# Every third lower weight part on Pool instead of DVE, in the first two blocks of a three-block model

## The chip, the cores and the metric

The kernel runs on one core of a Trainium2 chip. TensorE (PE) multiplies matrices, VectorE (DVE), ScalarE (ACT) and GpSimd (Pool) do elementwise work, and SyncE (SP) issues most transfers. The metric is the device time of one execution in microseconds; a median of several runs is compared with another.

## The reference

256 tokens of width 1024 in float32 pass through three blocks. The first has a gated recurrence, causal attention and a gated feed-forward part; the second has two kinds of attention and a table lookup ("peer": for each token 128 rows of a table of 16,384 are gathered); the third has a long convolution and 16 experts. Cut to what matters here, the first block's products with weights are:

```python
u = jnp.einsum('bsd,de->bse', h, w_in[l])                # 1024 x 7168
merged = (gates[:, :, 0] * jnp.einsum('bsc,cd->bsd', ya, w_proj_rnn[l])
          + gates[:, :, 1] * jnp.einsum('bsc,cd->bsd', yb, w_proj_attn[l]))
x = x + jnp.einsum('bsd,de->bse', merged, w_out[l])
up = causal_dwconv(jnp.einsum('bsd,df->bsf', h, w_up[l]), ffn_conv_w[l], ffn_conv_b[l])
act = jax.nn.gelu(up) * jnp.einsum('bsd,df->bsf', h, w_gate[l])
x = x + jnp.einsum('bsf,fd->bsd', act, w_down[l])
```

The second block opens with `mod = jax.nn.silu(c) @ ada_w[l] + ada_b[l]` and has the same kind of products with its own `w_in`, `w_out` and `wq`; the third has a like vector from `mod_w`.

## The kernel before

A product with a float32 weight matrix is made of three products of a rounded type: each operand is split into an upper part (rounded to that type) and a lower part (what is left). A weight tile is 128 x 1024, 512 KB. `K.mm3` (lines 158 to 160) multiplies upper by upper, upper by lower and lower by upper, so one tile costs PE 24 matmuls of 256 columns or 12 of 512.

The tiles come through a ring of five (`RING`, tile name `wraw`), filled by SP in the order of one long list (`items`). An item is a weight tile or, spread between the weights, a tile of `ada_w` or `mod_w`, which DVE alone uses (lines 369 and 372: it is multiplied by a column and added up in a tile `mod`; line 357 ends such a sum after eight matmuls of line 355 on PE). `K._process` takes the next item. For a weight, ACT makes the upper part `whi` (line 108) and DVE the lower part, `wlo` = `wraw` - `whi` (line 112). Three pairs of parts are held (`SPLIT`); a pair comes free when PE has done with it, and a place of the ring when `wlo` or the sum of line 372 has been read from it. SP's next transfer for that place waits for it, and SP's queue is in order, so later transfers wait behind it.

`K.get` hands PE's code the next pair. Before it does, it calls `_process` until three pairs are there (one while `still` is set, at the ends of a block). In the steady state two are there and the third is made, so a tile is split two tiles ahead of its use. Then `get` runs what has been put off (`settle`: results taken from PSUM, convolutions, splits of activations) and one step of `bg`. Every engine runs its instructions in the order in which this code writes them.

Pool does little in the first two blocks: the second of the two tiles that `K.ahead` splits at four places (also line 112), two pairs of squares `qkT` = `qk` * `qk` in `qk_norm` (line 533), whose sums DVE takes at line 536 as steps of `bg`, and six additions into `x` (line 976). In the lookup behind the second block, Pool issues all gathers (line 1174).

The feed-forward loop of the first block does, for each of 11 steps, two tiles of `w_up`, two of `w_gate`, two of `w_down`; DVE runs a convolution (lines 752 and 755: `cv` from `up`), a product (line 760, from PSUM) and the lower part of `act` (line 269). In the other stretch that is spoken of below, the gates of the recurrence, DVE works on `xa`, `om` and the sums of `qkT`; line 516 is `xa` = (`th` + 1) * `xa`, line 514 ACT's `th`.

Of the kernel before, what the change touches and what calls it, by code (L numbers as in the profile page):

```python
# [39 lines left out]
class K:  # L40
# [5 lines left out]
    def __init__(self, ctx, tc, a):  # L46
        self.tc, self.nc, self.a = tc, tc.nc, a
        nc = tc.nc
        self.const = ctx.enter_context(tc.tile_pool(name="const", bufs=1))
        self.dram = ctx.enter_context(tc.tile_pool(name="dram", bufs=1, space=DRAM))  # L50
        self.ps = tc.alloc_tile_pool(name="ps", bufs=4, space=PSUM, reuse_waits="tile")
        self.x = self.const.tile([128, 2, 1024], F32, name="x")
        for t in range(2):
            nc.sync.dma_start(self.x[:, t], a["x"][t * 128:t * 128 + 128])
        self.ident = self.const.tile([128, 128], F32, name="ident")
        nc.scalar.dma_start(self.ident, a["ident"])
        self.cols = self.const.tile([128, NCOLS], F32, name="cols")
        nc.scalar.dma_start(self.cols, a["cols"])
        self.ones = self.const.tile([128, 128], F32, name="ones")
        nc.vector.memset(self.ones, 1.0)  # L60
        self.sums, self.sums_bufs = None, 2
        self.still = False
        self.consume_first = False
        self.bg = []
        self.post = []
        self.bg_rate = 1
        self.ring = tc.alloc_tile_pool(name="ring", bufs=self.RING, side="right", reuse_waits="tile")
        self.split_p = tc.alloc_tile_pool(name="splt", bufs=self.SPLIT, side="right", reuse_waits="tile")
# [45 lines left out]
    def get(self):  # L114

        n = self.loaded
        m = 1 if self.still else self.SPLIT
        if self.consume_first:
            self.settle()
        while self.done < len(self.items) and (not self.parts or self.done < n and len(self.parts) < m):  # L120
            self._process()
        self._load(self.done + self.RING)
        self.settle()
        for _ in range(self.bg_rate):
            if self.bg:
                self.bg.pop(0)()
        return self.parts.pop(0)
# [691 lines left out]
def block2(k, mod, M):  # L819
# [190 lines left out]
    p3 = [k.mm(), k.mm()]  # L1010
    k.rows_part(p3, yT, 2, 4)
    M.vectors(1)
    k.still = True
    k.rows_part(p2, yT, 3, 4)
    k.later(x_add, 1, 0, p2)
    k.rows_part(p3, yT, 3, 4)
# [1223 lines left out]
@with_exitstack  # L2240
def model_kernel(ctx: ExitStack, tc: tile.TileContext, a: dict, out: bass.AP):
    ctx.enter_context(tc.manual_schedule())
    k = K(ctx, tc, a)
    mod2, items2 = k.modulation(k.const, 2, k.col("c2", 0, 8), a["ada_w"], a["ada_b"])
    mod3, items3 = k.modulation(k.const, 3, k.col("c3", 0, 8), a["mod_w"], a["mod_b"])
    raw = items2 + items3
    k.start(plan1(a, raw[:40], raw[40:80]) + plan2(a, raw[80:]) + plan3(a))
    pc = tc.alloc_tile_pool(name="b2c", bufs=1, reuse_waits="tile")
    M = Columns(k, mod2, pc)
    block1(k, lambda: M.vectors(0))  # L2250
    pA = [tc.alloc_tile_pool(name="pA0", bufs=2, reuse_waits="tile")]
    normed_at = block2(k, mod2, M)
    pA.append(tc.alloc_tile_pool(name="pA1", bufs=2, reuse_waits="tile"))
    F = peer(k, mod2, pA, normed_at)
    block3(k, mod3, F, out)
    for z in pA[::-1] + [pc, k.ps]:
        z.release()
# [23 lines left out]
```

## Time and profile before

| | us |
|---|---|
| median of 3 runs | 2575.07 (2574.85 to 2579.13) |
| the profiled execution, whole | 2579.07 |
| its span in the profile | 2577.2 |
| first two blocks, up to the last addition into `x` | about 642 |
| first gather of the lookup | 674.5 |

| engine | busy us in the span | share |
|---|---|---|
| PE | 2063.1 | 80% |
| DVE | 1374.0 | 53% |
| ACT | 566.4 | 22% |
| Pool | 326.8 | 13% |

The shares are averages over stages that differ. Up to 640 us, PE and DVE are both busy nearly all the time. From 770 to 1,030 us the gathers of the lookup keep the DMA engines at about 420 GB/s, and from 1,675 us on the experts' weights do so at about 415 GB/s. DVE has almost nothing to do in the last 900 us. A time in the rows below counts from the start of the span.

### The profile page before, as it was taken

What the parts mean: (1) busy time and instruction counts of PE and PEld (TensorE: products, weight loads), DVE (VectorE), ACT (ScalarE), POOL (GpSimd) and SP (SyncE); (2) the same over time, 40 slices, a digit from 0 to 9 for tenths busy, and PEclk for the clock granted to TensorE, in tenths of its full rate; (3) what the DMA queues carried; (4) which work ended last, traced back from release to release, by engine and by line L of the source; (5) the groups of instructions that cost most, each with busy time, mean ns of one, the idle gap of its engine ahead of it and who ended that gap; (6) DMA issues with size and microseconds to landing.
All of it is one profiled execution on the core that took longest, in us unless ns stands there. A gap on an engine that the chain in (4) does not pass through costs nothing. (4 is left out here: it accounts for less than half of the span.)

```text
span 2577.2 us, 29437 instructions
## 1 busy us (share of the span) xinstructions
PE 2063.1 (80%) x11067; PEld 1200.5 (47%) x11067; DVE 1374.0 (53%) x2774; ACT 566.4 (22%) x998; POOL 326.8 (13%) x317
## 2 busy tenths in 40 slices
PE   8899999899797777788778797876776677676675
PEld 8699898787653232343333795321122111221221
DVE  8988788877778887998665888200000000000001
ACT  5654444455411111211110443000000000000000
POOL 0100000001224333233222123000000000000000
PEclk9999999999899999899889898688778878878788
DMA  7767688674699999999878448799999999999997
GB/s 261 232 219 259 207 308 302 229 260 145 263 381 421 421 421 419 368 371 387 315 297 340 108 137 314 290 415 414 415 415 414 414 415 415 415 414 417 415 414 290
DMA packets 188031, 860.85 MB, mean 334 GB/s; under 512 B 29945, under 2 KB 35121, under 8 KB 131057
## 3 DMA queue, kind: packets, MB, share of 16 engines
q1 hardware_dynamic: 137904, 578.19, 59.0%
q0 software_dynamic: 36864, 268.45, 25.8%
q10 hardware_dynamic: 13120, 12.32, 1.5%
q8 instruction: 88, 1.44, 0.2%
q14 instruction: 55, 0.44, 0.0%
HBM read 857.79 MB, written 1.10 MB: 333 GB/s over the span
## 5 line engine op out<-in xcount | busy, mean ns | idle before, releaser
L1927 DVE TENSOR_TENSOR xe<-mm,m 128x256 f32<-128x256 f32 x15 | 6.4, 425 | 602.4 <-PE mm L1925 602.4
L112 DVE TENSOR_TENSOR wlo<-wraw,whi 128x1024 fp32r<-128x1024 f32 x223 | 276.2, 1242 | 95.9 <-ACT whi L108 94.1
L108 ACT ACTIVATE whi<-wraw 128x1024 fp32r<-128x1024 f32 x228 | 239.5, 1056 | 177.9 <-PE mm L159 53.1
L1226 PE MATMUL ys<-G,diag 128*128 128x512 f32 x480 | 228.9, 617 | 50.7 <-DVE diag L1216 50.5
L1968 PE MATMUL mm<-K,xe 128*32 128x512 f32 x864 | 150.7, 697 | 78.9 <-DMA K<-in_moe_w_dram 78.9
L1968 PE MATMUL mm<-we,xe 128*32 128x512 f32 x864 | 146.9, 774 | 82.7 <-DMA we<-in_moe_w_dram 82.5
L158 PE MATMUL mm<-hTh,whi 128*128 128x256 f32 x608 | 173.2, 285 | 0.8 <-DVE hTl L306 0.8
L1226 PEld LDWEIGHTS ys<-G,diag 128*128 128x128 f32 x480 | 89.7, 195 | 178.7 <-issue 87.7
L160 PE MATMUL mm<-hTh,wlo 128*128 128x256 f32 x608 | 170.5, 280 | 0.0
L159 PE MATMUL mm<-hTl,whi 128*128 128x256 f32 x608 | 170.2, 280 | 0.0
L1200 DVE SCALAR_TENSOR_TENSOR G<-G,h 128x1024 f32<-128x1024 f32 x120 | 145.5, 1214 | 25.7 <-DMA G<-in_uv_dram,ids 25.3
L1226 PE MATMUL ys<-rowsS,diag 128*128 128x512 f32 x252 | 126.3, 641 | 36.3 <-DVE diag L1216 29.5
L1206 ACT ACTIVATE acts<-dots 128x2 f32<-128x2 f32 x128 | 26.0, 203 | 527.9 <-DVE G L1200 236.8
L1174 POOL DMA_INDIRECT G<-in_uv_dram,ids x120 | 115.4, 962 | 207.2 <-PE ys L1226 100.7
L1226 PE MATMUL ys<-rowsL,diag 128*128 128x512 f32 x168 | 96.5, 716 | 49.0 <-DVE diag L1216 48.6
L2035 DVE TENSOR_TENSOR ye<-mm,m 128x512 f32<-128x512 f32 x16 | 11.1, 692 | 213.9 <-PE mm L2029 213.9
L2071 POOL TENSOR_TENSOR x<-x,zT 128x512 f32<-128x512 f32 x1 | 1.6, 1551 | 962.7 <-ACT x L2070 962.7
L158 PEld LDWEIGHTS mm<-hTh,whi 128*128 128x128 f32 x608 | 115.4, 190 | 4.8 <-issue 2.0
L159 PEld LDWEIGHTS mm<-hTl,whi 128*128 128x128 f32 x608 | 116.2, 191 | 0.7
L1968 PEld LDWEIGHTS mm<-K,xe 128*32 128x32 f32 x864 | 22.8, 115 | 199.5 <-DMA K<-in_moe_w_dram 183.8
L160 PEld LDWEIGHTS mm<-hTh,wlo 128*128 128x128 f32 x608 | 115.3, 190 | 0.4 <-DVE wlo L112 0.2
L1968 PEld LDWEIGHTS mm<-we,xe 128*32 128x32 f32 x864 | 21.1, 121 | 202.4 <-DMA we<-in_moe_w_dram 181.1
(521 smaller groups left out, 4329.1 us busy)
## 6 DMA issues: line engine op xcount, KB each, us to landing
we<-in_moe_w_dram SPq DMA_DIRECT2D x160, 1024.0 KB
K<-in_moe_w_dram SPq DMA_DIRECT2D x122, 1024.0 KB
wraw<-in_moe_w_dram SPq DMA_DIRECT2D x100, 512.0 KB
K<-in_moe_w_dram SPq DMA_DIRECT2D x84, 512.0 KB
wraw<-in_w_in_dram SPq DMA_DIRECT2D x48, 512.0 KB
wraw<-in_ada_w_dram SPq DMA_DIRECT2D x48, 512.0 KB
wraw<-in_mod_w_dram SPq DMA_DIRECT2D x48, 512.0 KB
wraw<-in_w_qkv_dram SPq DMA_DIRECT2D x24, 512.0 KB
```

What stands on the lines that cost most here:

```text
L108: nc.scalar.activation(hi, raw, AF.Copy)
L112: (lower or nc.vector).tensor_sub(lo, raw, hi)
L158: nc.tensor.matmul(out, lhs[0], rhs[0], start=start, stop=False)
L159: nc.tensor.matmul(out, lhs[0], rhs[1], start=False, stop=False)
L160: nc.tensor.matmul(out, lhs[1], rhs[0], start=False, stop=stop)
L1174: nc.gpsimd.indirect_dma_start(out=z, out_offset=None, in_=a["uv"], in_offset=bass.IndirectOffsetOnAxis(ap=i[:, n % 16:n % 16 + 1], axis=0))
L1200: nc.vector.scalar_tensor_tensor(u, u, 1.0, h2[0], op0=ALU.mult, op1=ALU.mult, accum_out=dots[s][:, e:e + 1])
L1206: nc.scalar.activation(acts[s][:, e:e + 2], dots[s][:, e:e + 2], AF.Gelu)
L1226: nc.tensor.matmul(ys[0][:, 512 * j:512 * j + 512], d, rows[n][1][:, 1024 + 512 * j:1536 + 512 * j], start=n % 128 == 0, stop=n % 128 == 127)
L1927: nc.vector.tensor_mul(xe, p, m4.unsqueeze(2).to_broadcast([128, 8, 32]))
L1968: nc.tensor.matmul(p[32 * j:32 * j + 32], xe[:, c], w[j], start=c == 0, stop=c == 7)
L2035: nc.vector.tensor_mul(ye, p, m5)
```

## The change

`get` counts weight tiles, and when the count is a multiple of three and the tile is the third pair (split two tiles ahead), it has the lower part made by Pool. A flag turns this off near the end of the second block, before the lookup begins. The lines below the first edit move by one, those below `get` by five.

```diff
@@ -60,6 +60,7 @@
         self.still = False
+        self.turn, self.assist = 0, True
@@ -118,7 +119,11 @@
         while self.done < len(self.items) and (not self.parts or self.done < n and len(self.parts) < m):
-            self._process()
+
+            weights = self.items[self.done][1] is None
+            self.turn += weights
+            far = weights and self.turn % 3 == 0 and len(self.parts) == self.SPLIT - 1
+            self._process(lower=self.nc.gpsimd if far and self.assist else None)
@@ -1010,7 +1015,7 @@
     M.vectors(1)
-    k.still = True
+    k.still, k.assist = True, False
```

58 of the `wlo` instructions move from DVE's queue to Pool's; nothing else moves on any engine. They are 14 up to 160 us of the profile before, 13 from there to 297 us, 21 in the feed-forward part (297 to 487 us) and 10 in the second block.

Pool's queue around the squares of line 533, before (numbers behind a name tell tiles apart):

```order
L112 TENSOR_TENSOR wlo_137<-wraw_86,whi_136 128x1024
L533 TENSOR_TENSOR qkT_1000<-qk_700 128x1024 x2
L533 TENSOR_TENSOR qkT_1225<-qk_1001 128x1024 x2
L112 TENSOR_TENSOR wlo_3068<-wraw_2957,whi_3067 128x1024
L112 TENSOR_TENSOR wlo_5254<-wraw_5126,whi_5253 128x1024
```

The same place of Pool's queue after:

```order
L113 TENSOR_TENSOR wlo_900<-wraw_801,whi_899 128x1024
L113 TENSOR_TENSOR wlo_1005<-wraw_903,whi_1004 128x1024
L538 TENSOR_TENSOR qkT_1000<-qk_700 128x1024 x2
L113 TENSOR_TENSOR wlo_1082<-wraw_1008,whi_1081 128x1024
L113 TENSOR_TENSOR wlo_1155<-wraw_1085,whi_1154 128x1024
L538 TENSOR_TENSOR qkT_1225<-qk_1001 128x1024 x2
L113 TENSOR_TENSOR wlo_1269<-wraw_1158,whi_1268 128x1024
```

The first squares now stand behind `wlo_1005`, the second behind `wlo_1155`, and `wlo_1269` behind the second.

DVE's queue at the same place (about 89 to 102 us), before:

```order
L112 TENSOR_TENSOR wlo_945<-wraw_880,whi_944 128x1024
L516 SCALAR_TENSOR_TENSOR xa_210<-th_957,xa_210 128x512
L516 SCALAR_TENSOR_TENSOR xa_210<-th_968,xa_210 128x512
L516 SCALAR_TENSOR_TENSOR xa_210<-th_979,xa_210 128x512
L516 SCALAR_TENSOR_TENSOR xa_210<-th_990,xa_210 128x512
L112 TENSOR_TENSOR wlo_1005<-wraw_903,whi_1004 128x1024
L536 TENSOR_REDUCE qss_1010<-qkT_1000 128x8
L372 SCALAR_TENSOR_TENSOR mod_1024_870<-wraw_905,mod_t_81,mod_1024_870 128x1024
L112 TENSOR_TENSOR wlo_1028<-wraw_925,whi_1027 128x1024
```

And after:

```order
L521 SCALAR_TENSOR_TENSOR xa_210<-th_979,xa_210 128x512
L521 SCALAR_TENSOR_TENSOR xa_210<-th_990,xa_210 128x512
L541 TENSOR_REDUCE qss_1010<-qkT_1000 128x8
L377 SCALAR_TENSOR_TENSOR mod_1024_870<-wraw_905,mod_t_81,mod_1024_870 128x1024
L113 TENSOR_TENSOR wlo_1028<-wraw_925,whi_1027 128x1024
```

`wlo_1005` has left the queue, and the sum over `qkT_1000` stands right behind the work on `xa`.

DVE's queue in the feed-forward part (about 387 to 398 us), before:

```order
L112 TENSOR_TENSOR wlo_4180<-wraw_4068,whi_4179 128x1024
L760 TENSOR_TENSOR cv_4029<-cv_4029,mm_4094 128x512
L372 SCALAR_TENSOR_TENSOR mod_1024_4135<-wraw_4100,mod_t_83,mod_1024_4135 128x1024
L112 TENSOR_TENSOR wlo_4202<-wraw_4102,whi_4201 128x1024
L269 TENSOR_TENSOR actl_4187<-cv_4029,acth_4186 128x512
L372 SCALAR_TENSOR_TENSOR mod_1024_4135<-wraw_4143,mod_t_83,mod_1024_4135 128x1024
L112 TENSOR_TENSOR wlo_4227<-wraw_4145,whi_4226 128x1024
L372 SCALAR_TENSOR_TENSOR mod_1024_4135<-wraw_4183,mod_t_83,mod_1024_4135 128x1024
L112 TENSOR_TENSOR wlo_4260<-wraw_4205,whi_4259 128x1024
L112 TENSOR_TENSOR wlo_4293<-wraw_4207,whi_4292 128x1024
```

And after:

```order
L765 TENSOR_TENSOR cv_4029<-cv_4029,mm_4094 128x512
L377 SCALAR_TENSOR_TENSOR mod_1024_4135<-wraw_4100,mod_t_83,mod_1024_4135 128x1024
L113 TENSOR_TENSOR wlo_4202<-wraw_4102,whi_4201 128x1024
L274 TENSOR_TENSOR actl_4187<-cv_4029,acth_4186 128x512
L377 SCALAR_TENSOR_TENSOR mod_1024_4135<-wraw_4143,mod_t_83,mod_1024_4135 128x1024
L113 TENSOR_TENSOR wlo_4227<-wraw_4145,whi_4226 128x1024
L377 SCALAR_TENSOR_TENSOR mod_1024_4135<-wraw_4183,mod_t_83,mod_1024_4135 128x1024
L113 TENSOR_TENSOR wlo_4293<-wraw_4207,whi_4292 128x1024
```

`wlo_4180` and `wlo_4260` have gone to Pool; the rest keeps its order.

## Rows read from the trace of the kernel before

**Rows 1.** Stretch, busy us (x count) of PE, PEld, DVE, ACT, POOL, clock, DMA.

```profile
110.00:160.00 50.00, 44.55 (x337) 41.88 (x336) 47.82 (x63) 28.31 (x36) 5.02 (x2) 0.93 0.69 222
...
400.00:450.00 50.00, 49.21 (x351) 44.13 (x351) 44.95 (x52) 23.03 (x26) 0.00 (x0) 1.00 0.89 310
```

**Rows 2.** PE's waits up to 660 us: total us, times, longest us.

```profile
PE mm L355 <- DVE mod L372: 6.2, 3, 5.5
...
PE mm L159 <- DVE wlo L112: 3.1, 4, 1.2
...
PE mm L160 <- DVE wlo L112: 1.9, 2, 1.2
```

**Rows 3.** Groups by line and shape: busy us, mean ns, idle before.

```profile
L112 DVE TENSOR_TENSOR wlo<-wraw,whi 128x1024 fp32r<-128x1024 f32 x223 | 276.2, 1242 | 95.9 <-ACT whi L108 94.1 <-ACT acts L1206 1.2
...
L372 DVE SCALAR_TENSOR_TENSOR mod<-wraw,mod_t,mod 128x1024 f32<-128x1024 f32 x84 | 109.5, 1303 | 0.0
...
L112 POOL TENSOR_TENSOR wlo<-wraw,whi 128x1024 fp32r<-128x1024 f32 x4 | 11.0, 2748 | 376.6 <-ACT whi L108 219.2 <-DVE rsn L209 157.4
```

**Rows 4.** Timeline, Pool and DVE together: start us, us, engine, line.

```profile
121.66 5.02 POOL L533 TENSOR_TENSOR qkT<-qk 128x1024 f32<-128x1024 f32 x2 [27.74 <-PE mm L160]
...
122.08 2.85 DVE L112 TENSOR_TENSOR wlo<-wraw,whi 128x1024 fp32r<-128x1024 f32 x1
...
491.33 2.46 POOL L112 TENSOR_TENSOR wlo<-wraw,whi 128x1024 fp32r<-128x1024 f32 x1 [204.86 <-ACT whi L108]
...
491.49 3.39 DVE L372 SCALAR_TENSOR_TENSOR mod<-wraw,mod_t,mod 128x1024 f32<-128x1024 f32 x1
...
621.15 2.55 POOL L976 TENSOR_TENSOR x<-x,s 128x512 f32<-128x512 f32 x2 [127.36 <-DVE s L973]
...
621.65 0.47 DVE L306 SCALAR_TENSOR_TENSOR hT2l<-mm,cols,hT2h 128x256 fp32r<-128x256 f32 x1
```

**Rows 5.** Timeline around the first squares: Pool, ACT, DVE.

```profile
88.39 5.53 POOL L533 TENSOR_TENSOR qkT<-qk 128x1024 f32<-128x1024 f32 x2 [73.98 <-ACT qk L569]
...
94.56 1.57 ACT L514 ACTIVATE th<-mm,hb 128x256 f32<-128x256 f32 x4 [3.18 <-DVE xa L516]
96.00 2.96 ACT L108 ACTIVATE whi<-wraw 128x1024 fp32r<-128x1024 f32 x3
...
97.11 1.23 DVE L112 TENSOR_TENSOR wlo<-wraw,whi 128x1024 fp32r<-128x1024 f32 x1 [0.26 <-ACT whi L108]
98.25 1.21 DVE L536 TENSOR_REDUCE qss<-qkT 128x8 f32<-128x1024 f32 x1
```

**Rows 6.** PE's longest wait in the timeline, and the stretch behind it by busy time.

```profile
129.77 1.08 PE L355 MATMUL mm<-mod,ones 128*32 128x256 f32 x8 [5.45 <-DVE mod L372]
...
128.50:135.40 6.90, 5.63 (x29) 4.83 (x30) 6.87 (x10) 0.61 (x1) 0.00 (x0) 0.51 0.55 164
```

**Rows 7.** Timeline of the feed-forward part: ACT, DVE, SP's issues, PE.

```profile
386.11 2.01 ACT L108 ACTIVATE whi<-wraw 128x1024 fp32r<-128x1024 f32 x2 [2.44 <-PE ac L160]
...
387.20 1.23 DVE L112 TENSOR_TENSOR wlo<-wraw,whi 128x1024 fp32r<-128x1024 f32 x1 [2.06 <-ACT whi L108]
...
388.61 0.28 PE L160 MATMUL mm<-hTh,wlo 128*128 128x256 f32 x1
...
390.25 0.33 SPq L93 DMA_DIRECT2D wraw<-in_w_gate_dram  x1
...
394.99 1.06 ACT L108 ACTIVATE whi<-wraw 128x1024 fp32r<-128x1024 f32 x1 [4.01 <-DMA wraw<-in_w_gate_dram]
...
396.09 2.50 DVE L112 TENSOR_TENSOR wlo<-wraw,whi 128x1024 fp32r<-128x1024 f32 x2 [0.60 <-ACT whi L108]
...
397.34 1.60 SPq L93 DMA_DIRECT2D wraw<-in_w_up_dram  x2
...
397.37 0.39 PE L160 MATMUL mm<-hTh,wlo 128*128 128x256 f32 x1
```

**Rows 8.** Pool's first gather of the lookup in the timeline.

```profile
674.50 2.19 POOL L1174 DMA_INDIRECT early<-in_uv_dram,ids  x1 [26.51 <-DVE gz L1130]
```

## The prediction

> **What bounds the kernel now.** I read the busy time by stretch first. Up to 640 us PE is the engine that sets the pace: in the middle of the feed-forward part it is busy 49.2 of 50 us, with DVE at 45.0 beside it, and in the gates of the recurrence DVE, at 47.8 of 50, is the busier of the two and PE loses 5.5 us [rows 1]. Then I read what PE waits for. The waits that have to do with DVE's lateness are few: 6.2 us for a sum of `mod`, and 3.1 and 1.9 us for `wlo` [rows 2]. The longest single one is at 129.77 us, 5.45 us for a sum that stands in DVE's queue behind work that runs without a gap since 97 us; behind it PE's clock is granted at 0.51 (the 1.2 GHz level) for 6.9 us [rows 6], which costs some 3.4 us more. So a DVE that came sooner everywhere could give back 6.2 + 3.1 + 1.9 + 3.4, some 14 us, and no more, because everywhere else PE is at work.
>
> A microsecond gained or lost here reaches the end. The first gather is issued at 674.5 us after a wait for DVE's choice of rows [rows 8], which needs the result of the second block; the gathers and then the experts' transfers come one after the other behind it, and nothing among them runs to a clock of its own. I count every shift of PE's work before 640 us once, in full.
>
> **What the change moves, and the price of one.** 58 `wlo` leave DVE, at 1.24 us each (mean), 72 us of its queue. On Pool the same instruction takes 2.46 to 2.75 us [rows 3, 4]. Pool has room: 58 times 2.75 is 160 us of 640. The price lies elsewhere, in what DVE does meanwhile. At 122.08 us a `wlo` on DVE ran beside Pool's squares and took 2.85 instead of 1.24 us. At 491.49 a sum of `mod` ran beside a `wlo` on Pool and took 3.39 instead of 1.30. At 621.65 an instruction whose one input is in PSUM ran beside Pool's additions at 0.47 us, no longer than elsewhere [rows 3, 4]. So a DVE instruction that reads two SBUF tiles stands still behind Pool's, by 1.61 (2.85 - 1.24) to 2.09 us (3.39 - 1.30), and one that reads PSUM doesn't. Each moved `wlo` then saves DVE 1.24 us and costs it nothing to 2.09: between -1.24 and +0.85 us. In the queues shown with the change, most of what stands around a moved `wlo` reads two SBUF tiles: the other `wlo`, the sums of `mod`, the convolutions, line 516, the lower part of `act`. Where DVE is behind I take +0.4, from the lower of the two rows, which is the one where Pool had to let a DVE instruction finish first, as will be usual in a full queue.
>
> The Trainium skill, page "SBUF — State Buffer", section "Who interferes with whom", says that a DVE instruction with two SBUF inputs and a GpSimd instruction that reads SBUF exclude each other, and that the one that comes second blocks for the whole instruction of the first. By that rule a moved `wlo` would cost DVE up to the whole 2.46 to 2.75 us, +1.2 to +1.5 net, and by an estimate the sum of this text would come out some 11 us higher (14 moved before 160 us, 0.8 more each). The trace agrees in kind and shows somewhat less, 2.09 of 2.46 us [rows 4].
>
> A second price: Pool's part is ready 1.2 to 1.5 us later than DVE's where DVE would have begun at once, and the place in the ring comes free as much later. Behind it wait, in SP's queue, all later transfers.
>
> **Up to 160 us, 14 moved.** DVE is behind here, so the ledger of its queue up to the sum at 129.77 counts. The first squares on Pool now stand behind `wlo_1005`. Before, they ran at 88.39 and held up line 516, for which ACT waited 3.18 us at 94.56 [rows 5]. Without them there, the first `whi` of the row at 96.00 ends at about 93.8 instead of 97.1; Pool makes `wlo_1005` until 96.3 and the first half of the squares until 98.8, and DVE's sum over them, next in its queue, starts there, where it stood at 98.25 before: +0.55. What DVE saved by the moved `wlo` (97.11) and by the squares' absence it spends waiting for the squares. Their second half then holds the sum of `mod` behind: +1.2 (until 101.3, when it could start at 100.0). `wlo_1082` and `wlo_1155`: +0.4 each, rounded up to 0.9. `wlo_1269` stands on Pool behind the second squares (121.66 + 5.02), meets DVE's scans and the awaited sum, +1.6, while the `wlo` that it saves stands behind that sum. Together 4.2 us; I take **+3**, because some of these meetings will be missed. Bounds: -9 (the whole wait and the half clock gone, 5.45 + 3.4) and +6 (14 times 0.4).
>
> **160 to 297 us, 13 moved.** None of the six waits for `wlo` in rows 2 lies here, and PE works without a break; a part is made two tiles ahead, some 5.6 us at 2.8 us a tile, of which `whi` (1.06) and Pool (2.75) take 3.8. That cover hides Pool's extra 1.5: **0**, at most +1.
>
> **Feed-forward part, 21 moved.** Here the ring counts. One revolution can be followed in rows 7: a transfer issued at 390.25 has its `whi` start at 394.99, when it lands, its `wlo` starts at 396.09 and its place is refilled at 397.34, 7.1 us for five tiles. PE takes five tiles (3.1 weights, the rest being `ada_w` or `mod_w`) in 8.7 us at 2.8 us a weight (351 matmuls in 49.2 us, 20 to a weight on the average [rows 1]). That leaves 1.6 us a revolution. Each revolution will hold about one moved `wlo`, +1.2 to +1.5, and a DVE instruction behind it that loses 0.4 to 0.85: 1.6 to 2.35 against 1.6, so 0 to +0.75 each, 0 to +16 for all. Directly: the `wlo` at 387.20 would be ready at 389.66 to 389.95 instead of 388.43, where PE reads it at 388.61, so PE loses 1.05 to 1.35; the one at 396.09 is ready at 398.55 to 398.85, where PE reads it at 397.37, or about a microsecond later by then, so 0.2 to 0.7 more [rows 7]. Two more of the 21 are as tight; the other 17 leave Pool 2.7 us and more. I take 1 us for each of the four and a tenth for each of the others, **+6**.
>
> **Second block, 10 moved.** At two places PE already waits for a `wlo` that is late because its `whi` is (two of the six waits of rows 2): 1.2 us more at each, **+2**, between 0 and +3. At the other eight PE waits for no part. The flag lets Pool go before the lookup, so its gathers meet none of this.
>
> **The sum.** 3 + 0 + 6 + 2 = +11 us. Against the profiled execution's own 2579.07 us that is 2590; it lay 4.0 above the median of the runs, 2575.07, so the median after should be **2586 us**. The bounds together are -14 (rows 2 and 6 all returned, no new wait) and +26.
>
> **Rivals.** First, faster: DVE's relief wins. It does if Pool's work falls mostly where DVE reads PSUM, waits or has nothing to do. DVE's 94 us of waiting for `whi` before a `wlo` speak for this [rows 3]: a moved `wlo` no longer blocks what stands behind it. Against it: in the stretch where PE loses most, DVE does not wait. From about 0.85 us of blocking downward per moved `wlo` the ledger turns; then the wait at 129.77 shrinks below what lets the clock fall, and 8 to 14 us come back: about 2564.
>
> Second, no change: PE covers it all. It is so if the ring keeps 1.6 us a revolution and the gates come out even: 2575, give or take 5.
>
> Third, much slower: the ring becomes the bound of the whole feed-forward part. It decides from 1.6 us of delay per revolution; with every revolution paying 0.75 and DVE's queue paying its upper price of 0.85 before 160 us, 16 + 12 + 3, less what is counted in both, some +28: 2603. The page's rule named above leads the same way.
>
> **How the numbers follow.** A difference of 0.2% (5 us) is about what a measurement of this kernel can tell from none. The forecast (2581 to 2598) gets 0.51, the third rival 0.09, no change 0.21, faster 0.19. So slower 0.60, same 0.21, faster 0.19. For 8 in 10 the range has to take in no change and part of faster: 2566 to 2602; the forecast's own is 2581 to 2598.
>
> **What would show it.** `wlo` on Pool at 2.4 to 2.8 us, 62 of them. On DVE, sums of `mod` and `wlo` up to 640 us that last 2 to 3.4 us instead of 1.24 and 1.30, in numbers of the order of 40; DVE's busy time up to 640 us not lower by 72 us but about the same. DVE's sum of line 536 (now 541) idle before it, waiting for Pool. PE's wait for the sum of `mod` near 130 us at 7 to 9 us instead of 5.45, and the first gather at about 685 instead of 674.5 us. In the feed-forward part, SP's transfers waiting for Pool, and PE waits of a microsecond for Pool's `wlo`. I am wrong if DVE's instructions keep their durations (then Pool and DVE do not meet), or if the first gather comes before 674 us. I am wrong about the place, and perhaps right about the sign, if PE's waits behind 300 us do not grow.

## The result: slower by 0.95%, in the forecast's direction and about twice its size

The changed kernel took 2600.66 us (median of 4 runs, 2598.84 to 2603.48) against 2577.10 us of the kernel before (4 runs beside it, 2574.85 to 2579.37). The ratio is 1.0095, with a 95% interval of 1.0080 to 1.0109: some 24 us slower. Forecast were 11 us, a median of 2586. The range given for 8 chances in 10, 2566 to 2602, holds the result near its upper end; the forecast's own, 2581 to 2598, does not. The profiled execution took 2599.27 us.

Here are the groups of the changed kernel that answer to [rows 3], from the page of the profile (line, engine, operation, shapes, count | busy us, mean ns | idle before). Line 112 is now 113, line 372 is 377.

```profile
L113 DVE TENSOR_TENSOR wlo<-wraw,whi 128x1024 fp32r<-128x1024 f32 x165 | 222.8, 1355 | 77.8 <-ACT whi L109 76.0
L113 POOL TENSOR_TENSOR wlo<-wraw,whi 128x1024 fp32r<-128x1024 f32 x62 | 163.5, 2638 | 478.9 <-ACT whi L109 474.6
...
L377 DVE SCALAR_TENSOR_TENSOR mod<-wraw,mod_t,mod 128x1024 f32<-128x1024 f32 x84 | 141.7, 1686 | 8.3 <-DMA wraw<-in_mod_w_dram 6.2
```

DVE has 58 `wlo` less, yet the mean of those it keeps rose from 1242 to 1355 ns, and that of the sums of `mod` from 1303 to 1686. The engines' busy time in the whole execution (us, share of the span, instructions), of the kernel before and then of the changed one:

```profile
PE 2063.1 (80%) x11067; PEld 1200.5 (47%) x11067; DVE 1374.0 (53%) x2774; ACT 566.4 (22%) x998; POOL 326.8 (13%) x317
```

```profile
PE 2061.1 (79%) x11067; PEld 1201.0 (46%) x11067; DVE 1385.9 (53%) x2716; ACT 567.1 (22%) x998; POOL 477.0 (18%) x375
```

DVE has 58 instructions fewer and is busy 12 us longer. What PE waits for in that time, beside [rows 2] (waiting engine and line, releaser: us in total, times, longest):

```profile
PE mm L360 <- DVE mod L377: 9.2, 4, 7.4
PE mm L164 <- DVE wlo L113: 6.7, 3, 5.1
...
PE mm L165 <- DVE wlo L113: 4.3, 4, 3.1
PE mm L165 <- POOL wlo L113: 4.3, 6, 1.3
PE ac L164 <- DVE wlo L113: 3.8, 6, 1.5
...
PE mm L164 <- POOL wlo L113: 3.2, 2, 1.9
```

DVE's own instructions, more than Pool's, are what PE waits for longest. The place of the loss comes from setting the first use of each weight tile on PE in one trace beside the other's (PE's shift, one execution of each kernel). The changed kernel is behind by 1.7 us at 39 us (in the time of before), 3.5 at 66, 7.4 at 74.5, 11.1 at 104.5, 14.2 at 167; then nothing until 264, where it becomes 16.5; from 356 to 477 us it climbs from 17.2 to 26.0; it falls back to 23.2 behind 520 us. The first gather, [rows 8], is late by the same:

```profile
697.79 2.19 POOL L1179 DMA_INDIRECT early<-in_uv_dram,ids  x1 [26.51 <-DVE gz L1135]
```

### The profile page after: what moved, and what is told of

It is laid out like the page before. It is cut to its first block, busy times and chain, and to the rows that moved or that the text cites. A ratio compares the mean times of both kernels' runs of the same rounds, so it can differ in the third digit from the quotient of the medians.

```text
span 2597.5 us, 29443 instructions
## 1 busy us (share of the span) xinstructions
PE 2061.1 (79%) x11067; PEld 1201.0 (46%) x11067; DVE 1385.9 (53%) x2716; ACT 567.1 (22%) x998; POOL 477.0 (18%) x375
## 5 line engine op out<-in xcount | busy, mean ns | idle before, releaser
L113 DVE TENSOR_TENSOR wlo<-wraw,whi 128x1024 fp32r<-128x1024 f32 x165 | 222.8, 1355 | 77.8 <-ACT whi L109 76.0
L113 POOL TENSOR_TENSOR wlo<-wraw,whi 128x1024 fp32r<-128x1024 f32 x62 | 163.5, 2638 | 478.9 <-ACT whi L109 474.6
L377 DVE SCALAR_TENSOR_TENSOR mod<-wraw,mod_t,mod 128x1024 f32<-128x1024 f32 x84 | 141.7, 1686 | 8.3 <-DMA wraw<-in_mod_w_dram 6.2
L1231 PE MATMUL ys<-rowsL,diag 128*128 128x512 f32 x168 | 90.7, 679 | 48.4 <-DVE diag L1221 48.4
L2040 DVE TENSOR_TENSOR ye<-mm,m 128x512 f32<-128x512 f32 x16 | 11.1, 692 | 212.9 <-PE mm L2034 212.9
```

The source lines that it names most:

```text
L113: (lower or nc.vector).tensor_sub(lo, raw, hi)
L377: nc.vector.scalar_tensor_tensor(z, raw, th[:, ch:ch + 1], z, op0=ALU.mult, op1=ALU.add)
L1231: nc.tensor.matmul(ys[0][:, 512 * j:512 * j + 512], d, rows[n][1][:, 1024 + 512 * j:1536 + 512 * j], start=n % 128 == 0, stop=n % 128 == 127)
```

## Hold-ups: what they look like

Three places of the changed kernel's timeline, Pool's `wlo` first and DVE's instruction beside it second (start us, us, engine, line):

```profile
38.43 2.86 POOL L113 TENSOR_TENSOR wlo<-wraw,whi 128x1024 fp32r<-128x1024 f32 x1 [5.29 <-ACT whi L109]
...
38.94 3.43 DVE L377 SCALAR_TENSOR_TENSOR mod<-wraw,mod_t,mod 128x1024 f32<-128x1024 f32 x1
...
66.97 2.41 POOL L113 TENSOR_TENSOR wlo<-wraw,whi 128x1024 fp32r<-128x1024 f32 x1 [6.91 <-ACT whi L109]
...
67.04 2.89 DVE L274 TENSOR_TENSOR yRl<-xa,yRh 128x512 fp32r<-128x512 f32 x1
...
571.80 2.38 POOL L113 TENSOR_TENSOR wlo<-wraw,whi 128x1024 fp32r<-128x1024 f32 x1 [11.06 <-ACT whi L109]
...
572.26 1.95 DVE L884 TENSOR_SCALAR m<-m 128x2 f32<-128x2 f32 x1
```

The sum of `mod` takes 3.43 instead of 1.28 us; `yRl` 2.89 where it takes 0.68 alone, and ten instructions later in DVE's queue stands a `wlo` for which PE waits 3.13 us (at 76.09); an instruction on two columns takes 1.95 where it takes 0.17. I added up, over all DVE instructions that overlap one on Pool up to 655 us, the duration less the median of the same form elsewhere (for three `yRl`, the 0.68 us of the kernel before): 10.9 us before, 90.5 after, of which 29.7 up to 172 us (6.7 before), 17.3 up to 310 (2.1), 35.2 up to 520 (2.1), 8.3 behind that (0.0). 55 instructions lost more than half a microsecond (6 before). That is 80 us of new hold-up for 72 us of relief (58 times 1.24), 1.37 us for each moved `wlo`.

## The experiments

The theories: **hold-up** (Pool's long read stops DVE instructions that read SBUF), **lateness** (a part made by Pool is ready later, and PE and the ring wait for it), and **queue** (Pool's squares stand behind a `wlo`, and DVE waits for them). Differences are of medians, in us against the runs of the kernel before on the same chip; the 95% interval of the ratio stands beside it. In the expectations TensorE is PE, VectorE DVE and ScalarE ACT.

### Does the loss add up by stretches?

One line before the loop behind the first 165 us (`k.assist = False`) leaves the first 14 moved parts:

```
+    k.assist = False
     prob = {}
```

> Pool's help is switched off before the feed-forward part's and the second block's share: only the first 14 moved lower parts (up to about 165 us) stay on Pool. By the profile after, TensorE's weight tiles stand 14 us later there, and by the theory that each lower part on Pool holds up a VectorE instruction beside it, and that this delay is local and never given back, the kernel comes to +12 to +15 us on the kernel before. The rival that the delay is only moved (the stretches behind would have waited anyway, and after's loss comes from the feed-forward part) gives +0 to +5 us.

Measured: +12.9 us (1.0038 to 1.0065). PE's weight tiles stand 14.9 us behind at 167 us and 15.0 at 666: nothing is given back. The other run turns the flag on for the feed-forward part of the first block alone:

```
-        self.turn, self.assist = 0, True
+        self.turn, self.assist = 0, False
     acts = {}
+    k.assist = True
     for r in range(11):
...
     last()
-    k.still = True
+    k.still, k.assist = True, False
```

> Pool helps in the 21 tiles of the feed-forward part of the first block alone. Local and additive losses: +7 to +9 us on the kernel before (after's shift grows from 16.2 to 24.5 us there). The ring-bound theory of the prediction with its own sizes: +6. If after's loss in the feed-forward part hangs on the kernel having come late into it (a ring still empty from the first stretch): +0 to +3.

Measured: +8.4 us (1.0023 to 1.0050). The two together are 21 of the 24; the feed-forward part loses its share although the kernel comes into it on time.

### Hold-ups without relief, and lateness without hold-ups

DVE keeps every `wlo`; Pool does an idle subtraction beside it, in five pieces:

```
+        if lower is not None and beside:
+            for h in range(5):
+                a = hi[:, 192 * h:192 * h + 192].bitcast(F32)
+                lower.tensor_sub(self.idle, a, a)
+            lower = None
         (lower or nc.vector).tensor_sub(lo, raw, hi)
```

> VectorE keeps every lower part, and Pool does an idle subtraction of the same kind beside it at the same 58 places (five pieces of 192 columns that read the upper part twice, into a scratch tile that nothing reads). Nothing of the kernel waits for Pool's result; only VectorE's relief is missing. By the theory of hold-ups (Pool's long reads of SBUF stop VectorE's instructions that read SBUF): at least after's loss, +24 to +45 us on the kernel before, and VectorE instructions of 2 to 3.5 us beside Pool's pieces. By the theory of lateness (a lower part made by Pool is ready later, and TensorE and the ring wait for that): 0 to +5 us.

Measured: +32.4 us (1.0112 to 1.0143). No product needs Pool's pieces here and DVE has no relief, and PE loses more than in the changed kernel. The timeline shows how DVE is held up, Pool first:

```profile
50.05 5.17 POOL L117 TENSOR_TENSOR idle<-whi 128x192 f32<-128x192 f32 x4
...
49.52 1.00 DVE L280 TENSOR_TENSOR yRl<-xa,yRh 128x512 fp32r<-128x512 f32 x1
50.44 1.52 DVE L119 TENSOR_TENSOR wlo<-wraw,whi 128x1024 fp32r<-128x1024 f32 x1
51.88 1.52 DVE L383 SCALAR_TENSOR_TENSOR mod<-wraw,mod_t,mod 128x1024 f32<-128x1024 f32 x1
```

Four pieces, 0.51 us each when alone, take 5.17 us: one piece runs between each two DVE instructions. A `wlo` takes 1.52 instead of 1.22 us, and Pool's piece waits meanwhile. They take turns. But two other effects are in these 32 us, so the run shows that hold-ups cost PE time and not how much they cost alone. Pool's squares stand behind the pieces, and DVE and PE behind the squares:

```profile
103.91 3.74 POOL L544 TENSOR_TENSOR qkT<-qk 128x1024 f32<-128x1024 f32 x2
...
105.84 1.22 DVE L547 TENSOR_REDUCE qss<-qkT 128x8 f32<-128x1024 f32 x1 [4.60 <-POOL qkT L544]
...
110.23 0.80 PE L170 MATMUL mm<-wlo,hTh 128*128 128x512 f32 x1 [5.91 <-DVE wlo L119]
```

And ACT waits three times, 13.5 us in all, until the pieces have read the upper part whose place it needs.

The opposite: the part is as late as Pool would have it, but nothing long is read.

```
+        if lower is not None and beside:
+            lower.tensor_sub(self.idle[:, 0:16], hi[:, 0:16].bitcast(F32), hi[:, 0:16].bitcast(F32))
+            for _ in range(5):
+                lower.memset(self.idle, 0.0)
+            lower.memset(lo.bitcast(F32), 0.0)
+            lower.tensor_sub(lo[:, 0:16], raw[:, 0:16], hi[:, 0:16])
+            return
```

> The same 58 lower parts come from Pool, at least as late as in the changed kernel, but without a long read of SBUF: Pool reads 16 columns of the upper part, fills scratch and the lower part with zeros, and subtracts 16 columns. The lower parts of these tiles are therefore zero but for 16 columns. By the theory of hold-ups: VectorE is relieved of 58 instructions and held up by none, -12 to +5 us on the kernel before, unless the fills themselves stop VectorE, which its durations beside them would show. By the theory of lateness: after's loss or more, +20 to +35 us.

Measured: +6.0 us (1.0013 to 1.0032), a microsecond over the first bound and far from the second. Pool's eight instructions for a part took 3.56 us on the average here, gaps included, where the changed kernel's one takes 2.64. So the run was repeated with two fills in place of five, which takes 2.64 us too (the expectation puts the first at 3.3):

> The changed kernel with zero fills in place of the long subtraction at all 58 places, cut to its length (about 2.5 us, where the run before had 3.3 us). The lower parts of these tiles are zero but for 16 columns. Relief and lateness without hold-ups at the changed kernel's own lateness. By the sum of the runs so far (relief alone -15.5 us, relief with 3.3 us of lateness +5.7): lateness in proportion to its length gives 0 to +2 us on the kernel before, so that hold-ups are 22 us of the changed kernel's 24. If lateness has a threshold (a part is in time or is not): as before, +5 to +7.

Measured: -3.9 us (0.9975 to 0.9995), better than either expected. DVE and Pool in this run, by line and shape up to 655 us:

```profile
L121 DVE TENSOR_TENSOR wlo<-wraw,whi 128x1024 fp32r<-128x1024 f32 x121 | 149.7, 1239 | 87.8 <-ACT whi L110 85.8 <-PE mm L173 1.5
L385 DVE SCALAR_TENSOR_TENSOR mod<-wraw,mod_t,mod 128x1024 f32<-128x1024 f32 x84 | 109.9, 1308 | 11.1 <-DMA wraw<-in_mod_w_dram 7.6 <-DMA wraw<-in_ada_w_dram 3.4
...
L118 POOL MEMSET wlo<- 128x1024 f32 x58 | 55.7, 960 | 0.0
```

The durations of DVE are those of [rows 3]: fills on Pool hold up nothing (12.5 us by the sum used above, 10.9 before). At the changed kernel's lateness and relief, without hold-ups, the kernel is 3.9 us faster than before instead of 24 slower. These parts are zeros but for 16 columns, and PE might have run faster on zeros; it did not: up to 640 us the clock was granted at 0.98 in both runs, and the matmuls of `hTh` and `wlo` took 280 ns here and 282 in the changed kernel. **Hold-ups are some 28 us of the result**, and lateness is steep: 0.9 us more for each part made 10 us of difference.

The third corner, relief alone:

```
+        if lower is not None and beside:
+            self.parts[-1] = (hi, hi)
+            return
         (lower or nc.vector).tensor_sub(lo, raw, hi)
```

> The 58 moved lower parts are made by nobody: TensorE multiplies with the upper part in their place, so these products are missing from the result. VectorE is relieved as in the changed kernel, Pool holds nobody up and no part comes late. By the reading that the run with zero fills left relief and lateness alone (TensorE 3.5 us ahead of the kernel before at 165 us, then 12 us lost to late parts): -4 us by 165 us and nothing lost later, in all -3 to -12 us on the kernel before. The rival that the loss behind 165 us comes from something else that the skipped VectorE work changes (ring and DMA order): +3 to +8 us again.

Measured: -15.6 us (0.9927 to 0.9954), more than expected. PE is 8.3 us ahead at 163 us, 15 at 483 and 19 at 640: DVE's relief is worth some 6 us in the feed-forward part too, where I had thought PE alone set the pace, and some 4 in the second block. (A place in the ring also comes free sooner here, since no `wlo` reads the tile; the run doesn't part the two.) So the changed kernel's +24 are -16 of relief, +12 of lateness (from this run to the zero fills of 2.64 us; the squares that queue behind Pool's part are in it), +28 of hold-ups, each worked out as the difference of two runs.

And lateness without hold-ups in the feed-forward part alone (the flag as in the second run, the zero fills in place of the subtraction):

> Pool helps in the 21 tiles of the feed-forward part alone, as in the run before that lost 9 us, but with the zero fills in place of the long subtraction, cut to about its length (2.5 us): late parts without hold-ups. The lower parts of these tiles are zero but for 16 columns. If the feed-forward loss is lateness (the part made by Pool comes later and TensorE and the ring wait): +5 to +9 us on the kernel before. If it is hold-ups of VectorE there: -4 to +2 us.

Measured: +4.5 us (1.0012 to 1.0032). That is half of the +8.4; the intervals overlap, so by the times alone hold-ups' share there, about 4 us, is likely but not settled. PE's waits in the changed kernel agree with it (313 to 505 us, where it does this part):

```profile
PE mm L165 <- POOL wlo L113: 4.3, 6, 1.3
PE ac L164 <- DVE wlo L113: 3.8, 6, 1.5
PE mm L360 <- DVE mod L377: 1.8, 3, 1.0
...
PE mm L165 <- DVE wlo L113: 0.5, 1, 0.5
```

The kernel before had none for Pool here, and 1.5 us (1.2 and 0.3) for DVE's `wlo` and sums.

### One operand instead of two, and halves

The idle pieces with one operand from SBUF:

```
-                lower.tensor_sub(self.idle, a, a)
+                lower.tensor_scalar_add(self.idle, a, 1.0)
```

> As the run in which VectorE keeps its lower parts and Pool does idle pieces beside it (+33 us), but each piece reads one operand from SBUF (adds a constant to 192 columns) where it read two. If any read of SBUF by Pool stops VectorE: +20 to +33 us on the kernel before, and VectorE's instructions stretched to about 1.5 us beside a piece. If it takes two operands of Pool: 0 to +5 us, and VectorE's durations as in the kernel before.

Measured: +12.3 us (1.0039 to 1.0066), between the two. DVE's `wlo` beside a piece mostly takes 1.36 to 1.38 us, 0.14 to 0.16 more than alone, against 0.30 with two operands: the hold-up is about half and not gone. Most of the 12 us have another cause, which stands out in this run. Pool's squares, DVE's sum over them, and PE:

```profile
95.84 4.82 POOL L117 TENSOR_SCALAR idle<-whi 128x192 f32<-128x192 f32 x5 [5.83 <-ACT whi L110]
100.63 3.74 POOL L544 TENSOR_TENSOR qkT<-qk 128x1024 f32<-128x1024 f32 x2
...
102.56 1.22 DVE L547 TENSOR_REDUCE qss<-qkT 128x8 f32<-128x1024 f32 x1 [5.54 <-POOL qkT L544]
...
106.79 0.79 PE L170 MATMUL mm<-wlo,hTh 128*128 128x512 f32 x1 [6.14 <-DVE wlo L119]
```

The squares stand behind Pool's other work, DVE's queue stands behind them for 5.54 us, and PE 6.14 us behind DVE. PE's shift goes from -0.7 to 7.5 us at this one place.

Halves, so that a DVE instruction waits for half as long:

```
+            for s in (slice(0, 512), slice(512, 1024)):
+                lower.tensor_sub(lo[:, s], raw[:, s], hi[:, s])
+            return
```

> The changed kernel with each of the 58 lower parts on Pool cut into two halves of 512 columns. The idle pieces showed Pool and VectorE taking turns: a VectorE instruction waited for one piece at most, and Pool's next piece waited for that instruction. If the hold-up of one VectorE instruction by one long Pool instruction is the price: half of it, but parts later by one VectorE instruction (about 1.2 us) where both are busy, +12 to +20 us on the kernel before. If turns only move the wait from VectorE to Pool's part: +22 to +30.

Measured: +30.6 us (1.0101 to 1.0132), worse than the whole. One place, Pool first:

```profile
75.89 3.66 POOL L115 TENSOR_TENSOR wlo<-wraw,whi 128x512 fp32r<-128x512 f32 x2 [6.23 <-ACT whi L109]
...
76.11 2.30 DVE L117 TENSOR_TENSOR wlo<-wraw,whi 128x1024 fp32r<-128x1024 f32 x1
78.33 2.30 DVE L381 SCALAR_TENSOR_TENSOR mod<-wraw,mod_t,mod 128x1024 f32<-128x1024 f32 x1
```

Each half holds up one DVE instruction by a microsecond (2.30 for 1.22, 2.30 for 1.28), and the second half waits for the DVE instruction between: 3.66 us for the part instead of 2.64. Over all parts, the hold-ups sum to 77 us instead of 90.5, but a part takes 3.35 us instead of 2.64: which suggests that more is lost in lateness than is saved in hold-ups.

### The other direction: Pool with less

If hold-ups are that dear, the long instructions that Pool has in the kernel before should cost too. The squares of the query and key rows, on ACT:

```
-            nc.gpsimd.tensor_mul(tok(T)[:, t], raw[:, t], raw[:, t])
+            nc.scalar.activation(tok(T)[:, t], raw[:, t], AF.Square)
```

> The kernel before with the four squares of the query and key rows on ScalarE instead of Pool. If Pool's squares hold up VectorE's long sums around 97 us and 125 us and so make TensorE's wait of 5.45 us before 130 us with the half clock behind it: -4 to -9 us. If ScalarE's four additional instructions (about 1.05 us each by its 128x1024 forms) delay the upper parts as much: -1 to +4 us.

Measured: -7.3 us (0.9961 to 0.9982), **faster than both kernels**. PE's wait for the sum of `mod` [rows 6] is shorter, and the clock behind it isn't lowered (1.00 where it was 0.51):

```profile
123.45 0.64 PE L355 MATMUL mm<-mod,ones 128*32 128x256 f32 x8 [2.08 <-DVE mod L372]
...
122.50:129.40 6.90, 5.95 (x55) 5.54 (x56) 6.87 (x9) 1.94 (x3) 0.00 (x0) 1.00 0.61 206
```

The same edit in the changed kernel:

> The changed kernel with the same four squares on ScalarE. If the jump of 6 us at 104.5 us comes from the chain of the prediction (squares queued behind a lower part on Pool, VectorE's sum of squares waiting for them, the next lower part late): that jump goes, and the kernel stands +13 to +19 us over the kernel before in place of +24. If it comes from the hold-up of VectorE's own instructions by the other lower parts on Pool: within 3 us of the changed kernel, +21 to +27.

Measured: +20.7 us (1.0065 to 1.0092), at the border of the two expectations; its interval and that of the changed kernel overlap. The jump at 104.5 us is gone, so the queue theory is right about that place. But PE now waits 3.31 us at 151.77 for a `wlo` of DVE's, in a row behind a DVE multiplication that Pool's part at 142.44 stretched from 0.68 to 2.88 us, and behind that wait the clock is granted at 0.50 for 6.8 us:

```profile
142.60 2.88 DVE L624 TENSOR_TENSOR om<-om,th 128x512 f32<-128x512 f32 x1
...
142.44 2.49 POOL L113 TENSOR_TENSOR wlo<-wraw,whi 128x1024 fp32r<-128x1024 f32 x1 [7.75 <-ACT whi L109]
...
151.10:157.90 6.80, 6.13 (x29) 6.14 (x30) 6.80 (x7) 2.24 (x4) 3.42 (x1) 0.50 0.52 154
```

Last, with the squares on ACT, the four `wlo` that the kernel before gives to Pool in `ahead` go to DVE too:

```
-            self._process(lower=self.nc.gpsimd if self.parts else None)
+            self._process()
```

> The kernel before with the squares on ScalarE, as in the run that gained 7 us, and the lower parts of the stretches that are split ahead on VectorE too (4 that the kernel before gives to Pool), so that Pool does no long subtraction in the first two blocks. If every long subtraction on Pool costs more in hold-ups than it saves: -8 to -12 us on the kernel before. If those 4 stand where VectorE's relief of 1.24 us each is worth more: -2 to -7 us.

Measured: -12.2 us (2563.93 us, 0.9945 to 0.9973), the fastest version of all that leaves nothing out; the step from the -7.3 of the squares alone is inside the intervals. Nothing long is left on Pool, and DVE is held up by nothing. PE's wait for the sum of `mod`, [rows 6], and the stretch behind it:

```profile
124.74 0.64 PE L355 MATMUL mm<-mod,ones 128*32 128x256 f32 x8 [2.07 <-DVE mod L372]
...
123.50:130.40 6.90, 5.66 (x38) 5.25 (x39) 6.87 (x10) 1.43 (x2) 0.00 (x0) 0.75 0.67 212
```

2.07 us instead of 5.45, as with the squares alone, and a clock of 0.75 instead of 0.51. Relief of DVE didn't do that: in the runs with relief alone and with zero fills, the wait near 130 us was still 5.0 and 5.3 us.

## Why the prediction was right in direction and short in size

**Right: what happens.** All 62 `wlo` on Pool at 2.64 us on the average, in the range of 2.4 to 2.8; DVE's busy time up to 640 us about the same (525 us, 529 before); 33 `wlo` and sums of `mod` on DVE that last 2 us or more (3 before), of the order of the 40; DVE waiting for Pool's squares at line 541 (4.61 us); PE's wait for the sum of `mod` at 7.39 us, in "7 to 9"; PE's microseconds for Pool's part in the feed-forward part (six waits, 4.3 us, the longest 1.3). The first gather came at 697.79 us, not at about 685, which is the error in size again. The mechanism that decided is the one of the sum, hold-ups of DVE; the changed kernel beside the zero fills of the same length shows it.

**The mis-sized term: up to 160 us, +3 forecast, +14 measured** (12.9 as a run of its own). The price of one was not the fault: the net of 0.4 us means 1.64 us of hold-up each, and the 14 of this stretch had 23.0 (29.7 - 6.7), 1.64 each. Three things were.

First, the ledger begins with `wlo_1005`. Eight of the 14 parts stand before it (Pool starts them from 20.57 to 89.37 us), and the sum has no term for them. Their hold-ups, 15.6 us, did reach PE: it waited for DVE's `wlo` at four places up to 67 us, and 3.13 us at 76.09, where it had waited 1.19 before. At 85 us, before the squares, it was 7.4 us late.

Second, the ledger charged PE at one place alone, the sum at 129.77. That wait grew by 1.9 us (5.45 to 7.39). PE also stopped at 111.59, for 5.07 us, where it had waited 0.43 before.

Third, it counted the clock only behind the sum. Behind the waits at 76.09 and 111.59 it was granted at 0.50 (the 1.2 GHz level), where the kernel before had 1.00, and each time PE fell back by some 1.3 us more:

```profile
77.00:80.40 3.40, 3.40 (x17) 3.13 (x15) 3.40 (x2) 2.58 (x7) 1.88 (x1) 0.50 0.61 233
111.20:114.60 3.40, 3.01 (x7) 2.43 (x8) 3.26 (x8) 0.00 (x0) 0.00 (x0) 0.50 0.63 183
```

The chain of the squares was booked at 1.75 us (0.55 and 1.2). In the trace the squares start at 103.39, behind `wlo_1005`:

```profile
101.02 2.42 POOL L113 TENSOR_TENSOR wlo<-wraw,whi 128x1024 fp32r<-128x1024 f32 x1 [8.14 <-ACT whi L109]
103.39 3.75 POOL L538 TENSOR_TENSOR qkT<-qk 128x1024 f32<-128x1024 f32 x2
108.11 2.34 POOL L113 TENSOR_TENSOR wlo<-wraw,whi 128x1024 fp32r<-128x1024 f32 x1 [0.97 <-ACT whi L109]
...
105.33 1.22 DVE L541 TENSOR_REDUCE qss<-qkT 128x8 f32<-128x1024 f32 x1 [4.61 <-POOL qkT L538]
106.47 1.76 DVE L377 SCALAR_TENSOR_TENSOR mod<-wraw,mod_t,mod 128x1024 f32<-128x1024 f32 x1
108.15 3.38 DVE L113 TENSOR_TENSOR wlo<-wraw,whi 128x1024 fp32r<-128x1024 f32 x1
...
111.59 0.80 PE L164 MATMUL mm<-wlo,hTh 128*128 128x512 f32 x1 [5.07 <-DVE wlo L113]
```

DVE idles 4.61 us before the sum over the squares. It starts 7.1 us later than before (105.33 and 98.25), and PE was already 7.4 us late at 85: up to here the chain came out about as booked, and DVE's saved time did pay for the wait. What was booked too low stands behind it. The next `wlo` on Pool holds up just the `wlo` that PE stands waiting for, by 2.16 us where 0.4 was booked, and the 2.3 us by which PE had caught up meanwhile (a shift of 5.1 at 98 us) are lost again. The bound of +6 was 14 times the average price, and an average can't bound what falls on the instruction that is awaited.

**160 to 297 us, 0 forecast, +2 measured.** The cover of two tiles failed once: Pool's part at 277.08 took 3.10 us, and PE waited 1.95 for it. **Feed-forward part, +6 forecast, +8 measured**, in place, and in kind by half. The waits for Pool's part are 4.3 us, and the run without hold-ups there gives 4.5. The other half is PE's waits for held-up DVE instructions, 6.1 us instead of 1.5, for which the +6 (a microsecond for each of four parts and a tenth for each of the others) has no term. The ring shows no loss of its own: SP's transfers wait 41.5 us for Pool from 297 to 480 us, but 145 us for all together, as many as before, and PE waits for no upper part there. What was left out, too, is that relief alone would have brought 6 us here. **Second block, +2 forecast, -1 measured** by PE's shift, from 24.3 at 483 us to 23.2: PE waits 1.3 us for Pool's part at one place, where it had waited 0.8 for DVE's, and three waits of the kernel before (0.4 to 0.8 us) are gone.

**The rivals.** "Faster" needed at most 0.85 us of blocking for each moved `wlo` (it was 1.37) and a wait near 130 us that shrinks; relief alone leaves that wait at 5.0 us, so its reason fell, not only its size. Its ceiling of some 14 us fits what relief alone gave (15.6, by the interval 12 to 19), but not the place: by PE's shift 6 came from the feed-forward part and 4 from the second block, where "everywhere else PE is at work" had left nothing. "No change" is excluded by the interval. "Much slower", 2603, is nearer to the measured 2600.66 than the forecast, but by luck: it rested on up to 16 us from a ring that bounds the feed-forward part, which lost 8, and not through the ring. Its 12 us before 160 us, at 0.85 net for each part, are near the 13 to 14 measured, though the net price was 0.4.

The Trainium skill, page "SBUF — State Buffer", section "Who interferes with whom", was weighed in the prediction with an estimate of 11 us more than the sum. The measured time lies nearer to that total than to my sum, but not for its reason: the hold-ups before 160 us were 1.64 us for each part, not 2.46 to 2.75, and what the sum lacked were places. The same section says that `tensor_scalar` can enter a mode that takes the shared port, while a Pool instruction that only writes SBUF leaves DVE with two SBUF inputs alone. Both agree with the runs: the 128x2 instruction of 0.17 us that took 1.95, and the zero fills that held up nothing. The prediction had counted only instructions with two SBUF inputs.

## What to carry to other kernels

Before work goes from DVE to Pool, set what DVE saves (here 1.24 us) against what DVE's neighbours lose beside Pool's instruction (here 1.37 us on the average, up to 2.2), and follow every instruction that another engine awaits, not the average: one awaited `wlo`, behind squares for which DVE had to wait and then held up itself, kept PE waiting 5 us, and the clock was at half behind it. Pool was idle here and still not free to use; look for long two-operand instructions on Pool in the kernel as it is and try them on ACT. And a ledger should begin at the first moved instruction and be closed at each place where the fast engine waits, not at the longest wait alone.

## What the chip showed that I had not expected

Pool and DVE take turns instruction by instruction, and cutting Pool's work in pieces doesn't make it cheaper (+24 us whole, +31 in halves). A Pool instruction with one SBUF operand held up DVE's `wlo` by 0.14 to 0.16 us where one with two operands over the same 192 columns cost 0.30; fills held up nothing. A DVE instruction on two columns was held nearly as long (1.8 us) as one on 1024 (up to 2.2). And not every read is held up: the sum over the squares, 128x1024 from one tile, took 1.22 us beside Pool's squares at 105.33, and 1.21 in the kernel before, where Pool was idle.
